# One decoder block on one core: slot weights and scatter matrix from one product, four small moves around it

## Chip, cores and metric

The kernel runs on one core of a Trainium2 chip. The metric is the device time of one launch in microseconds (us), the median over runs; lower is better.

## What is computed

One decoder layer on 256 tokens of width 1024, in float32: attention with two kinds of heads, then a mixture of 16 experts (top group of four, top two experts in it), then a final RMSNorm. The change touches the second half only:

```python
h2 = rmsnorm(x, norm2_g[l]) * (1.0 + scale2) + shift2
y = hierarchical_moe(h2, ...)          # top-1 group, top-2 experts in it
x = x + gate2 * y
return rmsnorm(x, final_g)

for e in range(N_EXPERTS):
    act = jax.nn.silu(hf @ w_gate[e]) * (hf @ w_up[e])
    out = out + combine[:, e:e + 1] * (act @ w_down[e])
```

`gate2` is one row of 1024 numbers from the conditioning vector, `combine` is zero but for a token's two experts, and `w_gate`, `w_up` and `w_down` are 96 MB together.

## The kernel before

Tokens stand in two tiles of 128 (t = 0, 1). After the router (lines 1059 to 1111) every expert has 64 slots, and the experts are worked through in eight pairs (p = 0 to 7, the loop at line 1359), a pair filling 128 slot rows. What a token's slot is stands in `onehot` (tokens x slots, zeros and ones, line 1190).

For each pair TensorE runs, in an order written by hand: the gate products (`in_half(p, "g", ...)`, line 1245) with the scatters of the pair before last between them, the up products, `slot_weights` (line 1256), the first half of the previous pair's down products (`down_rows`, line 1302), the transposes of the activations (`act_transpose`, line 1283), and the second half of the down products. After every odd pair `gather` (line 1200) fetches the tokens of the next four experts. Weights come by loads of 1 MB, all on the SP queue, into a ring of tiles (`st.tile`), many loads ahead of TensorE.

`slot_weights` makes two things for a pair. `sT` (slots x tokens) is the transpose of `onehot`, which later scatters the results back to the tokens; it is made by two TensorE transposes and copied out of PSUM by ScalarE. `ws` is one routing weight for each slot; it comes from two small float32 products of `onehot` with the routing weights `combv`, and two ScalarE copies. `weigh` (line 1320) multiplies a down product by `ws` and by the row `adaacc[5, n]` on VectorE and splits the result into a high part (`yh`) and a low part (`yl`); `scatter` (line 1338) multiplies them back into the accumulators `oacc`.

Three more places matter. `mod_rows(5)` (line 472) spreads the row `gate2` over all partitions, two float32 products and two ScalarE copies; it stands in pair 0, between `slot_weights` and `act_transpose`. `keep_clock` (line 167) issues bf16 products whose result nobody reads, three and four of them, while the router's small VectorE steps run. `final_row` (line 1132) spreads `final_g` over the partitions with eight small products and two ScalarE copies; it stands behind the last down products of pair 6. The end of the kernel is `norm_part` (line 1145, sums of squares on ScalarE and the product with `fg` on VectorE, by three column parts) and `norm_end` (line 1166): sum, power on GpSimd, scaling on ScalarE and VectorE, and four stores.

In the expert loop only TensorE's order is written by hand; in the router all of TensorE's, VectorE's and ScalarE's is. Elsewhere a scheduler sets it.

Of the kernel before, what the change touches and what calls it, by code (L numbers as in the profile page):

```python
# [61 lines left out]
def hybrid_block_kernel(  # L62
# [408 lines left out]

    def mod_rows(which):

        for j in range(2):
# [581 lines left out]
    weigh_logits(1)  # L1056
    keep_clock(3)

    larger = moe.tile([P, SETS, 16], F32, name="larger", bufs=1)
    G.memset(larger, 0.0)  # L1060
# [27 lines left out]
    h2_lo(0, 1)  # L1088
    keep_clock(4)

# [36 lines left out]
    PARTS = [slice(0, 512), slice(512, 768), slice(768, 1024)]  # L1127
    fgrow = small.tile([P, P], F32, name="fgrow", tag="lgs")[0:KD, :]
    nc.scalar.dma_start(fgrow, final_g.rearrange("(k p) -> k p", p=P))
    fg = []  # L1130
# [12 lines left out]
    norm = {}  # L1143

    def norm_part(i):
# [7 lines left out]
        for t in range(NT):  # L1153
            junk = act[:, 0:c.stop - c.start]
            S.activation(junk, oacc[t][n][:, cs], AF.Square, scale=D ** -0.5,
                         accum_out=ss[:, i, t:t + 1])
            if c is not PARTS[-1]:
                V.tensor_tensor(o[:, t, c], oacc[t][n][:, cs], fg[0][:, c], op=ALU.mult)
        if c is not PARTS[-1]:
# [6 lines left out]
    def norm_end():  # L1166
        o, ss = norm["o"], norm["ss"]
        c, cs = PARTS[-1], slice(PARTS[-1].start - FW, FW)
        r = small.tile([P, NT], F32, name="rstdf", tag="rstd")
        V.tensor_tensor(r, ss[:, len(PARTS) - 1, :], ss[:, len(PARTS) - 2, :], op=ALU.add)  # L1170
        G.tensor_tensor(r, r, mhalf, op=ALU.pow)
        for t in range(NT):
            rt_ = r[:, t:t + 1]
            S.mul(o[:, t, 0:512], o[:, t, 0:512], rt_)
            V.scalar_tensor_tensor(o[:, t, c], oacc[t][1][:, cs], rt_, fg[0][:, c], op0=ALU.mult,  # L1175
                                   op1=ALU.mult)
            V.tensor_scalar(o[:, t, 512:c.start], o[:, t, 512:c.start], rt_, None, op0=ALU.mult)  # L1177
            nc.scalar.dma_start(out[t * P:(t + 1) * P, 0:512], o[:, t, 0:512])
            nc.sync.dma_start(out[t * P:(t + 1) * P, 512:], o[:, t, 512:])
# [76 lines left out]
    def slot_weights(p):  # L1256

        lo = (2 * p) % 4
        oh = [onehot[p // 2 % 2][:, t, lo:lo + 2, :].rearrange("p e s -> p (e s)") for t in range(NT)]
        sp = psa(f"st{p}")  # L1260
        for t in range(NT):
            PE.transpose(sp[:, t * P:(t + 1) * P], oh[t].bitcast(F32), ident)
        for t in range(NT):
            PE.matmul(sp[:, T:T + NE], oh[t].bitcast(F32), combv[:, t, :], start=(t == 0),  # L1264
                      stop=(t == 1))
        sT = moe.tile([P, T], F32R, name="sT", tag="sT")
        S.copy(sT, sp[:, 0:T])  # L1267
# [69 lines left out]

    def scatter(yy, sT, n, cs):

        for y in yy:  # L1340
            for t in range(NT):
                m = sT[:, t * P:(t + 1) * P]
                PE.matmul(oacc[t][n][:, cs], m.bitcast(F32) if len(yy) == 1 else m, y, start=False,  # L1343
                          stop=True, skip_group_check=True)

    def scatter_pair(p, n, c):
        scatter(ys.pop((p, c.start)), sw[p][1], n, slice(c.start - FW * n, c.stop - FW * n))

    one_hot(0)
    for n in range(2):  # L1350
        h2_lo(1, n)
    combv = route_weights()
    by_hand.__exit__(None, None, None)
    NP = NE // 2
    whole_cols = [slice(0, FW), slice(FW, D)]
    with tc.manual_schedule(engines={PE.engine}):
        gather(0, 0)
        gather(0, 1)
        for p in range(NP):
# [17 lines left out]
            if p == 0:  # L1377
                mod_rows(5)
                nmaxi = most_tokens()
# [9 lines left out]
        load_down(p)  # L1389
        final_row()  # L1390
        scatter_pair(p - 1, 0, whole_cols[0])
# [14 lines left out]

    norm_end()

# [98 lines left out]
```

## Time and profile before

| | |
|---|---|
| median of three runs | 470.38 us (468.78 to 470.97) |
| the profiled execution, its own time | 470.29 us |
| its span, first to last instruction | 468.6 us |
| TensorE busy | 448.2 us, 96% |
| VectorE, ScalarE, GpSimd busy | 220.6, 160.6, 14.7 us |
| mean DMA rate | 338 GB/s |
| mean granted TensorE clock | 0.989 of 2.4 GHz |

The profile gives each instruction's start and length, what it waited for, and, by stretches, each engine's busy time, the granted clock (1.00 is 2.4 GHz, 0.50 is 1.2 GHz) and the DMA rate. A float32 product shows as two MATMUL rows. Since the ends of matmuls are modelled, the distance from one group's start to the next group's start tells more than their lengths.

### The profile page before, as it was taken

The numbers are of one execution on the slowest core, as the hardware profiler recorded it, in microseconds if no ns is written. First come the engines' busy times: TensorE is split into PE (matmuls) and PEld (weight loads), VectorE is DVE, ScalarE is ACT, GpSimd is POOL, SyncE is SP. The second block draws the span as 40 slices with busy tenths as digits, with TensorE's granted clock in tenths as the row PEclk, the third lists the DMA queues.
The fourth block names the chain that finished last, engine by engine and source line by source line (L and its number), as shares of the span: only waits on it lengthen the run. The fifth ranks groups of instructions, "written<-read, shape, count | busy, mean of one in ns | idle before, by whom it ended". The sixth has DMA issues, their size and how long they took to land. (4 is left out here: it accounts for less than half of the span.)

```text
span 468.6 us, 6867 instructions
## 1 busy us (share of the span) xinstructions
PE 448.2 (96%) x2724; PEld 281.2 (60%) x2724; DVE 220.6 (47%) x378; ACT 160.6 (34%) x292; POOL 14.7 (3%) x51
## 2 busy tenths in 40 slices
PE   5999999999999999999899999999999999999991
PEld 1769988976889999978453345333533335333440
DVE  5558878956999964787640030031202111020332
ACT  3543686465663444363641012011201102110222
POOL 5210000000000000000100000000000000000000
PEclk9999999999999999999999999999999999999986
DMA  8999978789797979976779999999999999999502
GB/s 290 368 324 354 295 267 287 247 287 382 254 374 255 385 263 407 422 308 219 294 258 408 424 420 418 422 419 421 420 421 419 422 419 421 420 420 404 196 0 94
DMA packets 51971, 158.46 MB, mean 338 GB/s; under 512 B 6448, under 2 KB 16728, under 8 KB 40160
## 3 DMA queue, kind: packets, MB, share of 16 engines
q1 hardware_dynamic: 51568, 157.44, 87.6%
q8 instruction: 23, 0.38, 0.3%
q10 hardware_dynamic: 368, 0.55, 0.3%
q14 instruction: 12, 0.10, 0.1%
HBM read 156.93 MB, written 1.05 MB: 337 GB/s over the span
## 5 line engine op out<-in xcount | busy, mean ns | idle before, releaser
L1252 PE MATMUL gps<-g,hg 128*64 128x512 f32 x256 | 57.9, 596 | 0.0
L1252 PE MATMUL ups<-u,hg 128*64 128x512 f32 x256 | 56.6, 595 | 0.0
L1309 PE MATMUL dps<-d,aT 128*64 128x512 f32 x224 | 51.2, 598 | 0.0
L1281 DVE TENSOR_TENSOR act<-act,ups 128x512 f32<-128x512 f32 x8 | 5.5, 687 | 93.6 <-PE ups L1252 93.6
L409 PE MATMUL g_acc<-hT,wsp 128*128 128x256 f32 x384 | 48.4, 285 | 0.3 <-DVE wsp L363 0.3
L409 PEld LDWEIGHTS g_acc<-hT,wsp 128*128 128x128 f32 x384 | 46.7, 191 | 1.6 <-issue 1.0
L1252 PEld LDWEIGHTS ups<-u,hg 128*64 128x64 f32 x256 | 17.9, 137 | 35.3 <-issue 35.3
L1252 PEld LDWEIGHTS gps<-g,hg 128*64 128x64 f32 x256 | 17.4, 137 | 33.2 <-issue 32.6
L1309 PEld LDWEIGHTS dps<-d,aT 128*64 128x64 f32 x224 | 14.8, 136 | 25.4 <-issue 25.2
L446 DVE SCALAR_TENSOR_TENSOR adarow<-adaw,cact,adarow 128x512 f32<-128x512 f32 x40 | 29.6, 743 | 0.4
L1327 ACT CAST yh<-yt 128x512 fp32r<-128x512 f32 x15 | 9.3, 618 | 56.7 <-DVE yt L1323 56.7
L1267 ACT CAST sT<-st 128x256 fp32r<-128x256 f32 x8 | 3.0, 372 | 63.4 <-PE st L1264 63.4
L940 PE MATMUL wo<-wsp,mT 128*128 128x512 f32 x96 | 23.7, 400 | 0.7 <-DVE wsp L363 0.7
L878 PE MATMUL br<-oT,wsp 128*128 128x256 f32 x192 | 23.2, 282 | 0.0
L1280 ACT ACTIVATE act<-gps 128x512 f32<-128x512 f32 x8 | 4.8, 598 | 53.7 <-PE gps L1252 53.7
L878 PEld LDWEIGHTS br<-oT,wsp 128*128 128x128 f32 x192 | 23.0, 188 | 0.2 <-DVE wsp L363 0.2
L1335 DVE TENSOR_TENSOR yl<-yt,yh 128x512 fp32r<-128x512 f32 x7 | 4.8, 692 | 34.3 <-PE oacc L1343 32.4
L940 PEld LDWEIGHTS wo<-wsp,mT 128*128 128x128 f32 x96 | 17.6, 188 | 5.2 <-DVE wsp L363 1.1
L1323 DVE SCALAR_TENSOR_TENSOR yt<-dps,ws,adarow 128x512 f32<-128x512 f32 (+1 forms) x17 | 12.2, 719 | 14.3 <-PE dps L1309 8.3
L1288 DVE COPY aT<-actT 128x512 f32<-128x512 f32 x8 | 5.5, 691 | 27.0 <-PE actT L1286 27.0
L1212 PEld LDWEIGHTS hg<-onehot,h2s 128*128 128x128 f32 x128 | 15.7, 191 | 4.2 <-ACT yh L1327 2.4
L1212 PE MATMUL hg<-onehot,h2s 128*128 128x256 f32 x128 | 16.8, 287 | 1.0 <-DVE h2s L1012 0.5
(295 smaller groups left out, 679.4 us busy)
## 6 DMA issues: line engine op xcount, KB each, us to landing
g<-in_expert_w_gate SPq DMA_DIRECT2D x32, 1024.0 KB, 14.6
u<-in_expert_w_up SPq DMA_DIRECT2D x32, 1024.0 KB, 16.3
d<-in_expert_w_down SPq DMA_DIRECT2D x30, 1024.0 KB, 17.2
adaw<-in_ada_w SPq DMA_DIRECT2D x16, 1024.0 KB, 6.4
ada<-in_ada_w SPq DMA_DIRECT2D x8, 512.0 KB, 8.9
ada<-in_ada_w SPq DMA_DIRECT2D x16, 256.0 KB, 8.5
wo<-in_w_out SPq DMA_DIRECT2D x4, 1024.0 KB, 12.9
kaw<-in_w_in SPq DMA_DIRECT2D x4, 512.0 KB, 6.6
```

Of the source, the lines that this page charges most:

```text
L409: PE.matmul(self.acc[m // 2][:, (m % 2) * T:(m % 2 + 1) * T], w[a][:, kk, m * P:(m + 1) * P], hT[b][:, k, :], start=(k == 0 and i == 0 and ...
L446: V.scalar_tensor_tensor(acc, adaw[which, j, k // 4][:, k % 4, :], cact[:, k:k + 1], acc, op0=ALU.mult, op1=ALU.add)
L878: PE.matmul(bacc[br][m // 2][:, (m % 2) * T:(m % 2 + 1) * T], wk[a][:, 0, m * P:(m + 1) * P], oT[br][b][:, k, :], start=(k == 0 and i == 0 ...
L940: PE.matmul(acc[t][n], mT[b][:, k, t * P:(t + 1) * P], ws[k // 2][a][:, k % 2, :], start=(k == 0 and i == 0), stop=(k == KD - 1 and i == 2))
L1212: PE.matmul(ps[:, kk * T:(kk + 1) * T], h2s[t][i][:, k * P:(k + 1) * P], oh[:, t].rearrange("p e s -> p (e s)"), start=(n == 0 and kk == 0 ...
L1252: PE.matmul(ps[64 * i:64 * i + 64, :], hg[:, k, (lo + i) * CAP:(lo + i + 1) * CAP], wt[nm, p][half][i][:, k % 4, :], start=(k == 0), stop= ...
L1280: S.activation(av, in_place(gu["g", p]), AF.Silu)
L1281: V.tensor_tensor(av, av, in_place(gu["u", p]), op=ALU.mult)
L1288: V.tensor_copy(aT, ap.rearrange("p (f s) -> p f s", f=KF))
L1309: PE.matmul(ys[p, FW * n][64 * i:64 * i + 64, :], aTs[p][:, 2 * h + k, 64 * i:64 * i + 64], dt_[p, h][i][:, k, FW * n:FW * n + FW], start= ...
L1323: V.scalar_tensor_tensor(y, ps, ws, adaacc[5, n][:, cs], op0=ALU.mult, op1=ALU.mult)
L1327: S.copy(hi, y)
```

## The change

A tile `wmove` is built once after the router: for each token tile 32 columns of routing weights, split in high and low parts, and one identity of 128 columns between them. `slot_weights` then needs one float32r product for each token tile, `onehot` times 160 columns of `wmove`, which gives the transpose and the weights together; two VectorE sums pick the weights of a pair out of them. Token tile 1 comes first in `sT`, so `scatter_pair` reads it in the order (1, 0). The two rows of `gate2` move to the places of `keep_clock(3)` and `keep_clock(4)`. `final_g` is spread over the partitions by one load on the SP queue behind the last weights. `norm_end` works by token tile, in an order written by hand, and the first half of tile 0's output is stored by the SP queue.

```diff
-    keep_clock(3)
+    mod_rows(5, (0,))
...
-    keep_clock(4)
+    mod_rows(5, (1,))
...
-    def final_row():
-        fg.append(st.tile("fg")[:, 0:D])
-        for n in range(2):
-            ps = psa(f"fg{n}")
-            for k in range(4):
-                PE.matmul(ps[:, k * P:(k + 1) * P],
-                          ident[0:KD, 4 * n + k:4 * n + k + 1].broadcast_to([KD, P]), fgrow,
-                          start=(k == 0), stop=True, skip_group_check=True)
-            S.copy(fg[0][:, 512 * n:512 * n + 512], ps)
...
-        V.tensor_tensor(r, ss[:, len(PARTS) - 1, :], ss[:, len(PARTS) - 2, :], op=ALU.add)
-        G.tensor_tensor(r, r, mhalf, op=ALU.pow)
         for t in range(NT):
+            V.tensor_tensor(rs[:, t:t + 1], ss[:, last, t:t + 1], ss[:, last - 1, t:t + 1],
+                            op=ALU.add)
+        for t in range(NT):
+            G.tensor_tensor(rs[:, t:t + 1], rs[:, t:t + 1], mhalf[:, 0:1], op=ALU.pow)
...
-            nc.scalar.dma_start(out[t * P:(t + 1) * P, 0:512], o[:, t, 0:512])
+            (nc.sync, nc.scalar)[t].dma_start(out[t * P:(t + 1) * P, 0:512], o[:, t, 0:512])
...
-        for t in range(NT):
-            PE.transpose(sp[:, t * P:(t + 1) * P], oh[t].bitcast(F32), ident)
-        for t in range(NT):
-            PE.matmul(sp[:, T:T + NE], oh[t].bitcast(F32), combv[:, t, :], start=(t == 0),
-                      stop=(t == 1))
+        PE.matmul(sp[:, 0:SW], oh[1], wmove[:, 2 * NE:2 * NE + SW], start=True, stop=True)
+        PE.matmul(sp[:, SW:2 * SW], oh[0], wmove[:, 0:SW], start=True, stop=True)
...
-            S.copy(ws[64 * i:64 * i + 64, :],
-                   sp[64 * i:64 * i + 64, T + 2 * p + i:T + 2 * p + i + 1])
+            V.tensor_reduce(ws[64 * i:64 * i + 64, :],
+                            sp[64 * i:64 * i + 64, P + 2 * p + i:P + 4 * NE:NE], axis=AX, op=ALU.add)
...
+    SW = P + 2 * NE
+    wmove = moe.tile([P, 2 * NE + SW], F32R, name="wmove", tag="wmove", bufs=1)
+    S.copy(wmove[:, 2 * NE:SW], ident)
...
-                mod_rows(5)
                 nmaxi = most_tokens()
                 act_transpose(p)
...
-        final_row()
+        fg = st.tile("fg")[:, 0:D]
+        nc.sync.dma_start(fg, final_g.unsqueeze(0).broadcast_to([P, D]))
```

The first place is TensorE in pair 0, from `slot_weights` to the first gate product of pair 1 (`st` holds the scatter matrix and the weights, `bc` the spread rows of `gate2`, `pmT` a transposed count, `actT` the transposed activations). Before:

```order
L1262 MATMUL st_2741<-ident,onehot_2618 128x128 x2
L1264 MATMUL st_2741<-rt_comb,onehot_2618 128x16 x2
L477 MATMUL bc_2751<-adarow_1597,onesr 128x512
L477 MATMUL bc_2754<-adarow_1608,onesr 128x512
L1119 MATMUL pmT<-ident,rt_pmax 1x128
L1286 MATMUL actT_2765<-ident,act 128x128 x4
L1252 MATMUL gps_2796<-g_0_2772,hg 64x512
```

With the change:

```order
L1253 MATMUL st_2742<-wmove,onehot_2613 128x160
L1254 MATMUL st_2742<-wmove,onehot_2613 128x160
L1120 MATMUL pmT<-ident,rt_pmax 1x128
L1276 MATMUL actT_2758<-ident,act 128x128 x4
L1242 MATMUL gps_2789<-g_0_2765,hg 64x512
```

Four instructions of `slot_weights` became two, and the two products of `mod_rows` are gone from here.

The second place is TensorE behind the last down product of pair 6 (`dps_1`); `oacc` are the scatters of pair 6 and `dps_3681` the first down product of pair 7. Before:

```order
L1309 MATMUL dps_1_3628<-d_1_3566,aT 64x512
L1138 MATMUL fg_3664<-fgrow,ident 128x128 x4
L1138 MATMUL fg_3670<-fgrow,ident 128x128 x4
L1343 MATMUL oacc_2533<-yh_2623,sT 128x512
L1343 MATMUL oacc_2567<-yh_2623,sT 128x512
L1343 MATMUL oacc_2533<-yl,sT 128x512
L1343 MATMUL oacc_2567<-yl,sT 128x512
L1297 MATMUL dps_3681<-d_0_3653,aT 64x512
```

With the change:

```order
L1299 MATMUL dps_1_3607<-d_1_3547,aT 64x512
L1333 MATMUL oacc_2533<-yh_2618,sT 128x512
L1333 MATMUL oacc_2567<-yh_2618,sT 128x512
L1333 MATMUL oacc_2533<-yl,sT 128x512
L1333 MATMUL oacc_2567<-yl,sT 128x512
L1287 MATMUL dps_3649<-d_0_3632,aT 64x512
```

The eight products of `final_row` no longer stand between the down products and the scatters.

The third place is VectorE from the weighing of pair 7's second part to the sums of the final norm (`ssf` are sums of squares, `o` the output before scaling). Before:

```order
L1323 SCALAR_TENSOR_TENSOR yt<-dps_3697,ws,adarow_1608 128x256
L1158 TENSOR_TENSOR o<-oacc_2533,fg 128x512
L1158 TENSOR_TENSOR o<-oacc_2567,fg 128x512
L1162 TENSOR_SCALAR ssf<-ssf 128x2
L1323 SCALAR_TENSOR_TENSOR yt<-dps_3718,ws,adarow_1608 128x256
L1158 TENSOR_TENSOR o<-oacc_2551,fg 128x256
L1158 TENSOR_TENSOR o<-oacc_2583,fg 128x256
L1164 TENSOR_TENSOR ssf<-ssf 128x2
L1170 TENSOR_TENSOR rstdf<-ssf 128x2
```

With the change:

```order
L1313 SCALAR_TENSOR_TENSOR yt<-dps_3665,ws,adarow_1608 128x256
L1148 TENSOR_SCALAR ssf<-ssf 128x2
L1144 TENSOR_TENSOR o<-oacc_2533,fg 128x512
L1144 TENSOR_TENSOR o<-oacc_2567,fg 128x512
L1313 SCALAR_TENSOR_TENSOR yt<-dps_3686,ws,adarow_1608 128x256
L1144 TENSOR_TENSOR o<-oacc_2551,fg 128x256
L1144 TENSOR_TENSOR o<-oacc_2583,fg 128x256
L1150 TENSOR_TENSOR ssf<-ssf 128x2
L1158 TENSOR_TENSOR rstdf<-ssf 128x1 x2
```

The small sum over `ssf` went ahead of the two products with `fg`, and the last sum is done once for each token tile.

## Rows read from the trace of the kernel before

**Rows 1.** Busy time by stretch: PE, PEld, DVE, ACT, POOL, clock, DMA, GB/s.

```profile
260.00:280.00 20.00, 20.00 (x98) 6.87 (x94) 2.90 (x6) 1.79 (x5) 0.00 (x0) 1.00 1.01 421
...
420.00:440.00 20.00, 20.00 (x94) 7.61 (x96) 2.43 (x4) 1.17 (x4) 0.00 (x0) 1.00 1.02 382
```

**Rows 2.** Timeline of PE, pairs 0 and 1: start, length, line, operation, shape, count.

```profile
254.63 0.44 PE L1262 MATMUL st<-ident,onehot 128*128 128x128 f32 x2
...
255.27 1.96 PE L477 MATMUL bc<-adarow,onesr 128*128 128x512 f32 x4
...
257.18 0.60 PE L1286 MATMUL actT<-ident,act 128*128 128x128 f32 x4
257.71 7.09 PE L1252 MATMUL gps<-g,hg 128*64 128x512 f32 x32
...
271.59 0.44 PE L1262 MATMUL st<-ident,onehot 128*128 128x128 f32 x2
...
272.31 3.65 PE L1309 MATMUL dps<-d,aT 128*64 128x512 f32 x16
...
280.07 4.09 PE L1212 MATMUL hg<-onehot,h2s 128*128 128x256 f32 x32
```

**Rows 3.** Issue of the second of the last weight loads, timeline of the SP queue.

```profile
415.19 1.13 SPq L1242 DMA_DIRECT2D d<-in_expert_w_down  x1
```

**Rows 4.** DMA issues from 414 to 417 us: count, size, us to landing.

```profile
d<-in_expert_w_down SPq DMA_DIRECT2D x1, 1024.0 KB, 20.4
```

**Rows 5.** Timeline of all engines behind the last down products of pair 6.

```profile
437.66 3.65 PE L1309 MATMUL dps<-d,aT 128*64 128x512 f32 x16
...
441.14 0.69 DVE L1330 TENSOR_TENSOR yl<-yt,yh 128x512 fp32r<-128x512 f32 x1 [0.74 <-ACT yh L1327]
...
441.25 2.05 PE L1138 MATMUL fg<-fgrow,ident 8*128 8x128 f32 x16
...
443.22 0.73 PE L1343 MATMUL oacc<-yh,sT 128*128 128x512 f32 x2
...
444.38 5.26 PE L1297 MATMUL dps<-d,aT 128*64 128x512 f32 x16
```

**Rows 6.** Timeline of all engines at the end.

```profile
454.33 1.41 DVE L1158 TENSOR_TENSOR o<-oacc,fg 128x512 f32<-128x512 f32 x2 [1.13 <-ACT act L1155]
...
454.82 0.19 ACT L1155 ACTIVATION_READ_ACCUMULATOR act<-oacc 128x1 f32 x1
...
455.76 0.48 DVE L1323 SCALAR_TENSOR_TENSOR yt<-dps,ws,adarow 128x256 f32<-128x256 f32 x1
...
457.39 1.21 PE L1343 MATMUL oacc<-yt,sT 128*128 128x256 f32 x4 [0.65 <-DVE o L1158]
...
459.44 0.70 POOL L1171 TENSOR_TENSOR rstdf<-rstdf,mhalf 128x2 f32<-128x2 f32 x1 [230.29 <-DVE rstdf L1170]
460.18 1.33 ACT L1174 ACTIVATE o<-o,rstdf 128x512 f32<-128x512 f32 x2 [1.00 <-POOLq L1411]
```

**Rows 7.** Timeline of all engines in pair 0, VectorE.

```profile
254.84 0.69 DVE L1281 TENSOR_TENSOR act<-act,ups 128x512 f32<-128x512 f32 x1 [13.53 <-PE ups L1252]
```

**Rows 8.** Timeline of all engines in the router, PE.

```profile
233.21 0.81 PE L171 MATMUL warm<-identb 128*128 128x512 bf16 x3
...
234.32 1.02 PE L171 MATMUL warm<-identb 128*128 128x512 bf16 x4
...
235.77 0.78 PE L1212 MATMUL hg<-onehot,h2s 128*128 128x256 f32 x3 [0.43 <-DVE onehot L1194]
```

**Rows 9.** Busy time, clock and DMA rate in two single microseconds, columns as in group 1.

```profile
443.00:444.00 1.00, 1.00 (x6) 0.77 (x5) 0.00 (x0) 0.97 (x3) 0.00 (x0) 1.00 0.00 0
...
445.00:446.00 1.00, 1.00 (x4) 0.24 (x2) 0.25 (x1) 0.00 (x0) 0.00 (x0) 0.50 0.00 0
```

**Rows 10.** Timeline of all engines in the router, GpSimd.

```profile
223.03 0.56 POOL L250 TENSOR_TENSOR rstd<-rstd,mhalf 128x1 f32<-128x1 f32 x1
```

**Rows 11.** All six last weight issues, timeline of the SP queue.

```profile
412.69 20.72 SPq L1242 DMA_DIRECT2D d<-in_expert_w_down  x6
```

More of the change, by code (lines that the diff above doesn't have):

```diff
@@ L470, in mod_split, with mod_rows @@
             msplit[which].append((hi, lo))
-    def mod_rows(which):
-        for j in range(2):
+    def mod_rows(which, js=(0, 1)):
+        for j in js:
             ps = psa(f"bc{which}{j}")
@@ L1056, in hybrid_block_kernel @@
     weigh_logits(1)
-    keep_clock(3)
-    larger = moe.tile([P, SETS, 16], F32, name="larger", bufs=1)
+    mod_rows(5, (0,))
+    larger = moe.tile([P, 192], F32, name="larger", tag="wmove", bufs=1)
+    larger = larger[:, 0:SETS * 16].rearrange("p (s c) -> p s c", s=SETS)
     G.memset(larger, 0.0)
@@ L1127, in hybrid_block_kernel @@
     PARTS = [slice(0, 512), slice(512, 768), slice(768, 1024)]
-    fgrow = small.tile([P, P], F32, name="fgrow", tag="lgs")[0:KD, :]
-    nc.scalar.dma_start(fgrow, final_g.rearrange("(k p) -> k p", p=P))
-    fg = []
-    def final_row():
-        fg.append(st.tile("fg")[:, 0:D])
-        for n in range(2):
-            ps = psa(f"fg{n}")
-            for k in range(4):
-                PE.matmul(ps[:, k * P:(k + 1) * P],
-                          ident[0:KD, 4 * n + k:4 * n + k + 1].broadcast_to([KD, P]), fgrow,
-                          start=(k == 0), stop=True, skip_group_check=True)
-            S.copy(fg[0][:, 512 * n:512 * n + 512], ps)
     norm = {}
@@ L1157, in norm_part @@
             if c is not PARTS[-1]:
-                V.tensor_tensor(o[:, t, c], oacc[t][n][:, cs], fg[0][:, c], op=ALU.mult)
+                V.tensor_tensor(o[:, t, c], oacc[t][n][:, cs], fg[:, c], op=ALU.mult)
         if c is not PARTS[-1]:
@@ L1168, in norm_end @@
         c, cs = PARTS[-1], slice(PARTS[-1].start - FW, FW)
-        r = small.tile([P, NT], F32, name="rstdf", tag="rstd")
-        V.tensor_tensor(r, ss[:, len(PARTS) - 1, :], ss[:, len(PARTS) - 2, :], op=ALU.add)
-        G.tensor_tensor(r, r, mhalf, op=ALU.pow)
+        rs = small.tile([P, NT], F32, name="rstdf", tag="rstd")
+        last = len(PARTS) - 1
         for t in range(NT):
-            rt_ = r[:, t:t + 1]
-            S.mul(o[:, t, 0:512], o[:, t, 0:512], rt_)
-            V.scalar_tensor_tensor(o[:, t, c], oacc[t][1][:, cs], rt_, fg[0][:, c], op0=ALU.mult,
+            V.tensor_tensor(rs[:, t:t + 1], ss[:, last, t:t + 1], ss[:, last - 1, t:t + 1],
+                            op=ALU.add)
+        for t in range(NT):
+            G.tensor_tensor(rs[:, t:t + 1], rs[:, t:t + 1], mhalf[:, 0:1], op=ALU.pow)
+        for t in range(NT):
+            r = rs[:, t:t + 1]
+            S.mul(o[:, t, 0:512], o[:, t, 0:512], r)
+            V.scalar_tensor_tensor(o[:, t, c], oacc[t][1][:, cs], r, fg[:, c], op0=ALU.mult,
                                    op1=ALU.mult)
-            V.tensor_scalar(o[:, t, 512:c.start], o[:, t, 512:c.start], rt_, None, op0=ALU.mult)
-            nc.scalar.dma_start(out[t * P:(t + 1) * P, 0:512], o[:, t, 0:512])
+            V.tensor_scalar(o[:, t, 512:c.start], o[:, t, 512:c.start], r, None, op0=ALU.mult)
+            (nc.sync, nc.scalar)[t].dma_start(out[t * P:(t + 1) * P, 0:512], o[:, t, 0:512])
             nc.sync.dma_start(out[t * P:(t + 1) * P, 512:], o[:, t, 512:])
@@ L1260, in slot_weights @@
         sp = psa(f"st{p}")
[L1261 to L1265 removed]
+        PE.matmul(sp[:, 0:SW], oh[1], wmove[:, 2 * NE:2 * NE + SW], start=True, stop=True)
+        PE.matmul(sp[:, SW:2 * SW], oh[0], wmove[:, 0:SW], start=True, stop=True)
         sT = moe.tile([P, T], F32R, name="sT", tag="sT")
[L1267 removed]
+        S.copy(sT.rearrange("p (t s) -> p t s", t=NT),
+               sp[:, 0:384].rearrange("p (t c) -> p t c", t=NT)[:, :, 0:P])
         ws = moe.tile([P, 1], F32, name="ws", tag="ws")
         for i in range(2):
[L1270 to L1271 removed]
+            V.tensor_reduce(ws[64 * i:64 * i + 64, :],
+                            sp[64 * i:64 * i + 64, P + 2 * p + i:P + 4 * NE:NE], axis=AX, op=ALU.add)
         sw[p] = ws, sT
@@ L1336, in weigh_low, with scatter @@
         ys[p, FW * n] = hi, yl
-    def scatter(yy, sT, n, cs):
+    def scatter(yy, sT, n, cs, order=(0, 1)):
         for y in yy:
             for t in range(NT):
-                m = sT[:, t * P:(t + 1) * P]
+                m = sT[:, order[t] * P:(order[t] + 1) * P]
                 PE.matmul(oacc[t][n][:, cs], m.bitcast(F32) if len(yy) == 1 else m, y, start=False,
@@ L1346, in scatter_pair @@
     def scatter_pair(p, n, c):
-        scatter(ys.pop((p, c.start)), sw[p][1], n, slice(c.start - FW * n, c.stop - FW * n))
+        scatter(ys.pop((p, c.start)), sw[p][1], n, slice(c.start - FW * n, c.stop - FW * n),
+                (1, 0))
     one_hot(0)
@@ L1352, in hybrid_block_kernel @@
     combv = route_weights()
+    SW = P + 2 * NE
+    wmove = moe.tile([P, 2 * NE + SW], F32R, name="wmove", tag="wmove", bufs=1)
+    S.copy(wmove[:, 2 * NE:SW], ident)
+    for t in range(NT):
+        hi, lo = (wmove[:, SW * t + NE * i:SW * t + NE * i + NE] for i in range(2))
+        S.copy(hi, combv[:, t, :])
+        V.tensor_tensor(lo, combv[:, t, :], hi.bitcast(F32), op=ALU.subtract)
     by_hand.__exit__(None, None, None)
@@ L1405, in hybrid_block_kernel @@
         norm_part(2)
-    norm_end()
+    with tc.manual_schedule(engines={V.engine, S.engine, G.engine}):
+        norm_end()
     nmaxv = nc.values_load(nmaxi[0:1, 0:1], min_val=0, max_val=T)
```

## Prediction

> **What bounds the kernel now.** I first read the busy time by stretch. From 260 to 440 us, the expert loop, TensorE is busy for the whole of every stretch, at a granted clock of 1.00, and the DMA queues move about 420 GB/s at a full busy share [rows 1]. Both look full, so the second view is the order in time: is TensorE waiting for weights? In the timeline of TensorE each group starts where the one before it ends: the up products of pair 1 give way to `slot_weights` at 271.59, that to the down products at 272.31, and so on [rows 2]. There is no gap that a load could explain. The third view is the loads: the second-last 1 MB load of the down weights is issued at 415.19 and lands 20.4 us later, at 435.6 [rows 3, 4]; TensorE first reads it at 444.4 [rows 5]. So weights lie ready 8.8 us ahead even at the end of the stream, and TensorE alone sets the pace from pair 0 to the last scatter. A microsecond taken off TensorE in that loop is a microsecond off the time, as long as the weights stay ahead. After it comes a chain of VectorE, TensorE, ScalarE, GpSimd and stores [rows 6], in which every link counts.
>
> **The rows of gate2 leave pair 0.** Before, the two products of `mod_rows` start at 255.27, the transposes of the activations at 257.18 and the next gate products at 257.71 [rows 2]. Without them the transposes would wait for their input, which VectorE ends at 254.84 + 0.69 = 255.53 [rows 7]. They take 257.71 - 257.18 = 0.53, so the gate products start at about 256.1: **1.6 us** earlier. The cheaper `slot_weights` of pair 0 is hidden in this wait. The rows go to the router in place of seven bf16 products that take 0.81 + 1.02 us [rows 8]; they cost 1.96 us for both [rows 2]. The second one has from 234.32 to the first gather at 235.77, which waits for VectorE's `onehot` [rows 8], and needs about 1.0: nothing. The first needs 1.0 where three products took 0.8, ahead of products that wait for the router's VectorE steps; at worst 0.2. I take 0 and keep 0.2 for the range. The ScalarE copies behind them fall into time in which it is idle, and so do the copies and subtractions that build `wmove`: nothing reads it before 254.6.
>
> **One product for each token tile.** `slot_weights` takes 272.31 - 271.59 = 0.72 us of TensorE before [rows 2]. What two float32r products of 160 columns take, no row shows. The nearest is the gather: float32r with 128 x 128 weights and 256 columns, 32 of them in 4.09 us, 0.13 each [rows 2]. Two such cost 0.26, and that saves 0.46 a pair. The other end is the rate of plain float32: each of the two products of `mod_rows` streams 512 columns in 1.96 / 2 = 0.98 us, so 160 columns cost 0.31 and two 0.61, saving 0.11 a pair. I take the gather's price, as type, weights and instruction are the same and only the columns differ. Seven pairs count (1 to 7): **3.2 us**, with 0.8 and 3.3 as ends. The Trainium skill, TensorE: Matmul & The Clock Gate, section The mechanism, speaks against so much: a weight load overlaps with a running matmul only where their row groups differ, which here they don't. By it and the skill's 128 / 1.2 ns for a load, an estimate, a gather product would need 0.21 and 32 of them 6.8 us; the trace has 4.09, so the row decides. By the rule the two products would cost 0.35, this term would be 2.6 and the time 462.3.
>
> The two weight copies move from ScalarE to VectorE sums; VectorE is busy 2.4 to 2.9 us in 20 [rows 1], and the weights are needed only by the weighing, several microseconds later: nothing.
>
> **final_row leaves TensorE.** Its products start at 441.25 and the scatters behind them at 443.22 [rows 5]: 1.97 us. In the new order the scatters follow the down products at once. Their first half has its input; the second needs `yl`, ready at 441.14 + 0.69 = 441.83, 0.58 behind 441.25, about as long as the first half takes. So the whole **1.97 us** goes, and all that came before shifts alike. The load that replaces it is 512 KB behind the last weights. At 382 GB/s [rows 1] that is 1.4 us; the old stream is at zero by 443 [rows 9], so it would land by 444.4, and VectorE's first product with `fg`, at 454.33 before [rows 6], comes at about 446.8 in the new time.
>
> **The clock.** Right behind `final_row` the granted clock falls from 1.00 to 0.50, that is from 2.4 to 1.2 GHz [rows 9], and the first down product of pair 7 takes 5.26 us for 16 rows, where the last of pair 6 took 3.65 for as many [rows 5]. What TensorE did before the fall is those small products, on 8 of its 128 rows, and scatters. Take the small ones away and only products of the kind that run all through the loop at full clock are left. I expect no fall: **1.6 us**. The other end is 0.
>
> **The end.** VectorE's two products with `fg` start at 454.33 today; in the new order a small sum stands ahead of them that waits for ScalarE's second sum, at 455.01 [rows 6]. They start some 0.85 later, and so does the weighing behind them (455.76), which then ends about 0.25 later than the products of the next part may start; the last scatters waited for those products at 457.39 [rows 6]. I charge 0.3. Against that the power: 0.70 for both tiles [rows 6], 0.56 for one [rows 10], and tile 0 no longer waits for tile 1's sum of squares, about 0.5. Scaling and stores then start 0.6 earlier. Net **0.3 us**, with -0.3 and 0.7 as ends.
>
> **Sum.** 1.6 + 3.2 + 1.97 + 1.6 + 0.3 = 8.7 us. The profiled execution took 470.29, so 461.6; it lies 0.1 below the median of the three runs, which makes 461.7.
>
> **Do the weights stay ahead?** By pair 7 TensorE is 1.6 + 3.2 = 4.8 us early, and the first down product there comes another 2.0 earlier: 444.4 - 6.8 = 437.6. The load it reads lands at 435.6. It holds by 2 us. The stream itself was at its full rate and does not move.
>
> **Rivals.**
> - *The new products are dear.* At the plain float32 rate the second term is 0.8: 461.7 + 2.4 = 464.1. For it: fewer columns than any float32r product of the trace. Against: the gather.
> - *Their weight loads are not hidden.* The old `slot_weights` was six short instructions, two transposes and two float32 products of two rows each, in 0.72 us, 0.12 each, whatever their columns. If each new product pays that and then streams 160 columns at the gather's rate, 0.08, two cost 0.40, a pair saves 0.32, and the term is 2.2: 462.7. For: the new products alternate with short work, as the old did. Against: in the gather 256 columns and a load fit into 0.13. It is the skill's rule above as a mechanism of this kernel.
> - *The clock still falls*, there or in the router, where seven bf16 products give way to two: 461.7 + 1.6 = 463.3. For: the fall came after little work, and scatters remain. Against: the same scatters stand in every pair, at a clock of 1.00.
> - *Weights become the bound.* If TensorE in truth follows the loads, the first two terms are hidden and only the last part is won: 461.7 + 4.8 = 466.5. For: 420 GB/s throughout. Against: 8.8 us of lead.
> - *Slower: `fg` arrives late.* The load is last in the SP queue; VectorE's product waits for it, the weighing stands behind that, TensorE behind the weighing. Every microsecond past 446.8 counts. The last weight issue ends at 412.69 + 20.72 = 433.4 [rows 11]; with the 20.4 us of a full queue it would land at 453.8, and the time would be 468.7. Only past 455.5 is it slower than before, by over 0.5% past 457.9. For: that queue is the slowest path here. Against: the old stream has run dry by 443, and 1.4 us of transfer follow.
>
> **Chances and range.** 0.5% (2.4 us) is about what can be told from no change. My forecast has 0.49; dear products 0.18; loads not hidden 0.08; the clock 0.12; weights 0.08; late `fg` 0.05, of which 0.03 ends within what can't be told and 0.02 past it. So faster 0.95, the same 0.03, slower 0.02. The range runs from 460.2 (the second term and the last at their ends, 0.5 together, and 1 us for the runs themselves, of which the lowest lay 1.6 under the median) to 464.6, which takes in the first three rivals and leaves out 0.13.
>
> **What would show it.** The next gate products about 1.6 us earlier behind pair 0; `slot_weights` at 0.25 to 0.3 us; no rows of `final_row`; clock 1.00 through the last down products; `fg` landing before VectorE asks for it; store issues about 8.7 us earlier. The prediction is wrong if TensorE shows waits for loads in pairs 1 to 7, if a product of 160 columns takes over 0.2 us, or if the clock falls anywhere between 230 us and the last scatter.

## The result, and the profile after

| | before | after | ratio, 95% interval |
|---|---|---|---|
| first timing, median | 470.41 us (468.78 to 470.97, 4 runs) | 463.54 us (461.32 to 464.56, 4 runs) | 0.9853 (0.9806 to 0.9900) |
| repeated, median | 468.90 us (22 runs) | 462.39 us (461.41 to 464.25, 6 runs) | 0.9858 (0.9835 to 0.9882) |
| profiled execution, its own time | 470.29 us | 461.32 us | |
| span | 468.6 us | 459.6 us | |
| mean granted clock of the span | 0.989 | 0.994 | |

The change is faster by some 1.4%, with the time inside the range that was given. In some executions of nearly every kernel here the mean granted clock of TensorE is lower than in the others (0.990 or less, not 0.991 to 0.995), and these take about 2 us longer; below, such an execution is said to have an extra fall of the clock. Of 49 executions of the kernel before, 19 were such by their times (470.3 to 471.0 us, against 468.5 to 469.1), and the one profiled ahead of the prediction was of this kind; of 10 of the changed kernel, 3 were (464.25 to 464.56). Like with like, by the medians of the executions without an extra fall, it is **468.8 against 462.3, so 6.5 us**. The forecast was 8.7 against 470.29.

The timeline of TensorE in pairs 0 and 1 after the change (start, length, line, operation, shape, count; L1253 and L1254 are the new products, L1299 the first half of pair 0's down products):

```profile
254.68 0.34 PE L1253 MATMUL st<-wmove,onehot 128*128 128x160 f32 x1
...
255.64 0.66 PE L1276 MATMUL actT<-ident,act 128*128 128x128 f32 x4 [0.40 <-DVE act L1271]
256.22 6.23 PE L1242 MATMUL gps<-g,hg 128*64 128x512 f32 x28
...
263.14 7.04 PE L1242 MATMUL ups<-u,hg 128*64 128x512 f32 x32
270.11 0.34 PE L1253 MATMUL st<-wmove,onehot 128*128 128x160 f32 x1
270.28 0.28 PE L1254 MATMUL st<-wmove,onehot 128*128 128x160 f32 x1
270.49 3.65 PE L1299 MATMUL dps<-d,aT 128*64 128x512 f32 x16
```

The gate products behind pair 0 start at 256.22 where they started at 257.71 [rows 2]: 1.49 earlier, with TensorE now waiting 0.40 for VectorE's `act`; the router gave up 0.05 of it, as `slot_weights` starts at 254.68 where it started at 254.63 [rows 2]. `slot_weights` takes 270.49 - 270.11 = 0.38, where it took 0.72 [rows 2].

The same view from the last down products of pair 6 on, and at the last scatters:

```profile
433.73 3.65 PE L1299 MATMUL dps<-d,aT 128*64 128x512 f32 x16
437.31 0.73 PE L1333 MATMUL oacc<-yh,sT 128*128 128x512 f32 x2
437.95 0.73 PE L1333 MATMUL oacc<-yl,sT 128*128 128x512 f32 x2
438.61 3.65 PE L1287 MATMUL dps<-d,aT 128*64 128x512 f32 x16
442.20 0.72 PE L1333 MATMUL oacc<-yh,sT 128*128 128x512 f32 x2
...
449.98 1.21 PE L1333 MATMUL oacc<-yt,sT 128*128 128x256 f32 x4 [0.65 <-DVE o L1144]
```

And its busy time by stretch there (PE, PEld, DVE, ACT, POOL, granted clock, DMA share, GB/s):

```profile
440.00:445.00 5.00, 5.00 (x32) 2.26 (x28) 1.63 (x3) 0.62 (x1) 0.00 (x0) 1.00 0.25 93
445.00:450.00 5.00, 4.35 (x29) 2.43 (x25) 2.66 (x6) 2.33 (x8) 0.00 (x0) 1.00 0.00 0
```

The down products of pair 6 start 437.66 - 433.73 = 3.93 earlier [rows 5]. No `final_row`; the first down product of pair 7 takes 3.65 and not 5.26 [rows 5], at a clock of 1.00. The scatters start 443.22 - 437.31 = 5.91 earlier, the last ones 457.39 - 449.98 = 7.41 [rows 5, 6]. The timelines of SP, VectorE, GpSimd and ScalarE at the end:

```profile
433.38 2.13 SPq L1390 DMA_DIRECT2D fg<-in_final_g  x1
...
437.21 0.69 DVE L1320 TENSOR_TENSOR yl<-yt,yh 128x512 fp32r<-128x512 f32 x1 [0.74 <-ACT yh L1317]
...
447.63 0.17 DVE L1148 TENSOR_SCALAR ssf<-ssf 128x2 f32<-128x2 f32 x1 [1.84 <-ACT act L1141]
447.70 1.28 DVE L1144 TENSOR_TENSOR o<-oacc,fg 128x512 f32<-128x512 f32 x2
448.90 0.48 DVE L1313 SCALAR_TENSOR_TENSOR yt<-dps,ws,adarow 128x256 f32<-128x256 f32 x1
449.50 0.93 DVE L1144 TENSOR_TENSOR o<-oacc,fg 128x256 f32<-128x256 f32 x2
...
451.52 1.06 POOL L1161 TENSOR_TENSOR rstdf<-rstdf,mhalf 128x1 f32<-128x1 f32 x2 [222.29 <-DVE rstdf L1158]
...
452.10 1.33 ACT L1164 ACTIVATE o<-o,rstdf 128x512 f32<-128x512 f32 x2 [0.35 <-POOL rstdf L1161]
```

VectorE's product with `fg` waits for ScalarE's sums (the small sum ahead of it, 447.63), not for the load of `fg`. Scaling starts at 452.10, where it was 460.18 [rows 6]: 8.08 earlier. From there to the end of the span it is 7.5 us, before 8.4; that last 0.9 was in no term of the forecast and is taken up below.

### The profile page after: what moved, and what is told of

It reads as the page before. It is cut to its first block, busy times and chain, and to the rows that moved or that the text cites. A ratio compares the mean times of both kernels' runs of the same rounds, so it can differ in the third digit from the quotient of the medians.

```text
span 459.6 us, 6762 instructions
## 1 busy us (share of the span) xinstructions
PE 440.5 (96%) x2669; PEld 275.1 (60%) x2669; DVE 223.5 (49%) x397; ACT 158.4 (34%) x277; POOL 15.1 (3%) x52
## 4 chain that ended last, share of the span: by engine, by line
PE 82%; DVE 8%; DMA 4%; ACT 2%; SPq 2%; issue 1%; POOL 0%; DVEq 0%; ACTq 0%
PE gps L1242 12%; PE ups L1242 12%; PE dps L1299 11%; PE g_acc L409 7%; PE wo L940 5%; PE br L878 4%; PE oacc L1333 4%; PE hg L1202 3%; PE vb_acc L401 3%; PE qb_acc L409 2%; PE kb_acc L409 2%; DMA ada<-in_ada_w 2%; DVE adarow L446 2%; PE ka_acc L409 2%; PE va_acc L401 2%; DMA qaw<-in_w_in 2%
## 5 line engine op out<-in xcount | busy, mean ns | idle before, releaser
L1299 PE MATMUL dps<-d,aT 128*64 128x512 f32 x224 | 51.1, 598 | 0.0
L1299 PEld LDWEIGHTS dps<-d,aT 128*64 128x64 f32 x224 | 14.8, 136 | 25.8 <-issue 24.8
```

The source lines that it names most:

```text
L1299: PE.matmul(ys[p, FW * n][64 * i:64 * i + 64, :], aTs[p][:, 2 * h + k, 64 * i:64 * i + 64], dt_[p, h][i][:, k, FW * n:FW * n + FW], start= ...
```

## The experiments

**The change once more, and each of three parts alone.** These four ran beside one set of runs of the kernel before. The first is the change unaltered.

> The changed kernel once more, unaltered, for its spread. In the profiled execution (461.3 us) the clock never fell before the end; two of the four timed ones had a lower mean clock (0.989, not 0.994) and took 464.4 to 464.6. Theory A, the clock still falls once in some executions at a place with little TensorE work: times in two clusters some 2 to 3 us apart, each with its own mean clock, about 461 to 463 and 464.5. Theory B, the spread is the DMA stream's or the launch's: times spread without any tie to the mean clock.

Measured: 462.39, ratio 0.9858 (0.9835 to 0.9882). Five of six executions stand at 461.41 to 462.54, one at 464.25 with a mean clock of 0.989. So theory A holds for the step of 2 us; the spread from 461.4 to 462.5 goes with no difference in the clock.

The kernel before with `final_g` by DMA alone:

```diff
-        final_row()
+        fg = st.tile("fg")[:, 0:D]
+        nc.sync.dma_start(fg, final_g.unsqueeze(0).broadcast_to([P, D]))
```

> The kernel before with one part of the change: final_g by one load, no products of final_row. Theory A, the small products cost TensorE's queue 1.97 us and their low work made the clock fall: 3.5 us less (466.9) where the clock stays up, 2.0 less (468.4) where it falls anyway. Rival, the fall has nothing to do with them: always 2.0 us less with the clock at 0.50 again in the first down product of pair 7.

Measured: 466.97, ratio 0.9958 (0.9942 to 0.9975). Against executions of before without an extra fall, 468.8, that is 1.9; two of twelve executions stand at 469.1 and 469.5 (mean clock 0.987 and 0.988), although `final_row` is gone.

The kernel before with the new `slot_weights`, `wmove` and the order (1, 0) in the scatters alone:

```diff
-        for t in range(NT):
-            PE.transpose(sp[:, t * P:(t + 1) * P], oh[t].bitcast(F32), ident)
...
+        PE.matmul(sp[:, 0:SW], oh[1], wmove[:, 2 * NE:2 * NE + SW], start=True, stop=True)
+        PE.matmul(sp[:, SW:2 * SW], oh[0], wmove[:, 0:SW], start=True, stop=True)
```

> The kernel before with one part of the change: one float32r product for each token tile. From the changed kernel's trace slot_weights takes 0.38 us where it took 0.72: theory, 7 x 0.34 = 2.4 us less (468.0), the whole of it visible since TensorE alone sets the pace. Rival, weights set the pace and it is hidden: 470.4. Pair 0 has no wait to hide it here, so up to 2.7 less.

Measured: 466.10, ratio 0.9935 (0.9912 to 0.9958), so 2.7 of 468.8. Here `final_row` remains, and yet the profiled execution has no fall behind it; nor has that of the next kernel, where it remains too. The timeline of TensorE in this one:

```profile
438.49 2.04 PE L1139 MATMUL fg<-fgrow,ident 8*128 8x128 f32 x16
...
441.59 3.65 PE L1298 MATMUL dps<-d,aT 128*64 128x512 f32 x16
```

The down product behind the eight products takes 3.65, and not the 5.26 of the kernel before [rows 5].

The kernel before with the rows of `gate2` in the router alone:

```diff
-    keep_clock(3)
+    mod_rows(5, (0,))
...
-    keep_clock(4)
+    mod_rows(5, (1,))
...
-                mod_rows(5)
```

> The kernel before with one part of the change: the rows of gate2 in the router in place of the seven bf16 products, nothing else. Theory, 1.5 us less (468.9), because pair 0 then waits 0.4 us for VectorE. Rival, the router loses what pair 0 wins (TensorE's clock falls there without the bf16 products): 470.4 or more, with the granted clock under 1.00 between 232 and 250 us.

Measured: 467.15, ratio 0.9965 (0.9947 to 0.9983), so 1.7. Three of eleven executions stand at 468.7 to 469.3 (mean clock 0.988 and 0.989).

What follows: `gate2` and `final_row` are worth what was forecast, the products less. And the clock's fall is an event of single executions, with `final_row` and without it. Two questions stayed: does `final_row` cause falls at all, and why do two products take 0.38?

**Does final_row make the clock fall?** The kernel before, with these products issued twice:

```diff
-            for k in range(4):
+            for k in list(range(4)) * 2:
```

> The kernel before with the eight small products that spread final_g issued twice, the second time with the same result. What is asked: whether these products, on 8 of TensorE's 128 rows, make the clock fall. The step of the prediction (they make it fall): the stretch of them is twice as long, so the clock falls right behind it in every execution; 468.85 + 1.97 for the products themselves + 1.6 for the fall = about 472.4, and the profile shows 0.50 from about 446 to 450 us. The rival (the fall is an event of single executions, wherever TensorE's products come from): 468.85 + 1.97 = about 470.8 for most executions, the profile mostly without a fall before the last scatter, and about one execution in four some 2 us higher, as in the kernel before.

Measured: 472.98 (472.27 to 473.80, 6 runs), ratio 1.0082 (1.0060 to 1.0103). No execution has a mean clock above 0.989; three stand at 472.3 to 472.5, where the step of the prediction put all of them, three another 1.3 higher. The stretch behind the doubled products, columns as above:

```profile
445.00:450.00 5.00, 5.00 (x19) 1.99 (x19) 0.69 (x1) 0.59 (x1) 0.00 (x0) 0.66 0.00 0
```

and TensorE's timeline there:

```profile
441.62 3.83 PE L1138 MATMUL fg<-fgrow,ident 8*128 8x128 f32 x32
...
446.51 5.35 PE L1297 MATMUL dps<-d,aT 128*64 128x512 f32 x16
```

Behind the doubled products on 8 of the 128 rows the clock is down at 1.2 GHz, 5.35 against 3.65 for the down product. By their mean clocks and times all six executions have a fall, though only one was profiled; behind the eight of the kernel before a fall stands in its one profile, and in neither profile of the two parts above that keep `final_row`. So the mechanism of the step holds; that it was there in every execution does not. What brought the second 1.3 us in three of the six no profile shows.

**Where do the longer executions of the changed kernel lose their 2 us?** The suspicion was the router. First, the change with both rows of `gate2` back in pair 0 and nothing in their place:

```diff
-    mod_rows(5, (0,))
...
-    mod_rows(5, (1,))
...
             if p == 0:
+                mod_rows(5)
```

> The changed kernel with both rows of gate2 back in pair 0 and no product in their place in the router, so that TensorE has nothing but the router's own short products for some 5 us there. What is asked: where the executions that are some 2 us longer lose that time. Theory A (the clock falls in the router, in some executions, because TensorE has little to do there): most or all executions are now in the longer group. Gate2 in pair 0 costs 1.7, the fall 2.0 to 2.5: 462.35 + 1.7 + 2.2 = about 466.3, and the profile shows a granted clock of 0.50 somewhere between 230 and 250 us. Theory B (the longer executions lose their time elsewhere): 462.35 + 1.7 = about 464.05 for most, a few 2 us above as before, and the clock is 1.00 from 230 us to the last scatter.

Measured: 465.88 (463.67 to 467.73, 7 runs), ratio 0.9932 (0.9908 to 0.9956); no execution has a mean clock above 0.989. The profile has the fall where theory A put it:

```profile
235.00:240.00 5.00, 3.65 (x17) 3.40 (x18) 3.97 (x11) 1.37 (x2) 0.00 (x0) 0.66 0.88 329
```

The gather and the products behind it in its timeline of TensorE:

```profile
237.08 4.91 PE L1200 MATMUL hg<-onehot,h2s 128*128 128x256 f32 x29 [0.49 <-DVE h2s L1012]
...
241.93 7.09 PE L1240 MATMUL gps<-g,hg 128*64 128x512 f32 x32
```

In this execution an idle router costs one fall, but only about 1.1 us (the first gate products at 241.93, in the changed kernel at 240.80); for a part of that time TensorE waits for VectorE. It is the fastest of the seven: the others stand 1.1 to 4.1 us higher, at mean clocks down to 0.981, and what more they lose no profile shows. Then, the change with eight more products that nobody reads:

```diff
     token_logits(0)
+    keep_clock(4)
...
     token_logits(1)
+    keep_clock(2)
...
     mod_rows(5, (1,))
+    keep_clock(2)
```

> The changed kernel with eight more bf16 products whose result nobody reads, in the router: four behind the first tile's logits, two behind the second's, two behind the second row of gate2. What is asked: whether filling TensorE there takes the longer executions away. If they come from a fall in the router: no execution above 463, all near 462.35 + 0 to 0.5 for what the products delay. If they come from elsewhere: about one in four stays 2 us higher, at about 464.4 or a little above.

Measured: 462.33 (461.35 to 463.24, 5 runs), ratio 0.9843 (0.9821 to 0.9865). One of the five, the profiled one, has the longer kind's clock, 0.990. Its stretches, columns as above, and its timeline of TensorE:

```profile
25.00:30.00 5.00, 3.31 (x17) 2.54 (x16) 4.10 (x9) 2.65 (x4) 0.00 (x0) 0.89 1.10 353
30.00:35.00 5.00, 5.00 (x32) 4.35 (x34) 1.94 (x3) 1.36 (x2) 1.06 (x2) 0.77 1.04 286
```

```profile
24.40 1.65 PE L401 MATMUL va_acc<-wsp,hT 128*128 128x512 f32 x6
27.74 1.05 PE L336 MATMUL adat<-fold,aacc 128*128 128x1 f32 x8 [1.69 <-DVE aacc L330]
28.65 2.67 PE L401 MATMUL va_acc<-wsp,hT 128*128 128x512 f32 x6
...
177.61 7.64 PE L878 MATMUL br<-oT,wsp 128*128 128x256 f32 x63
```

The same places in the changed kernel:

```profile
25.22 1.65 PE L401 MATMUL va_acc<-wsp,hT 128*128 128x512 f32 x6
26.71 0.95 PE L336 MATMUL adat<-fold,aacc 128*128 128x1 f32 x8
27.52 1.65 PE L401 MATMUL va_acc<-wsp,hT 128*128 128x512 f32 x6
...
175.56 9.66 PE L878 MATMUL br<-oT,wsp 128*128 128x256 f32 x80
```

In this execution TensorE came 0.8 us sooner to the `adat` products, waited 1.69 us for VectorE's `aacc`, and right behind that wait the clock was at 1.2 GHz for some 3 us: six products of 512 columns take 2.67 and not 1.65. About half of the loss is the wait itself (the `adat` products stand 1.03 later), the other half the clock (2.67 - 1.65 = 1.02). At 175 us it is 2.0 us late, and stays so. The edits of this kernel all lie behind 200 us. So here is one execution 2 us longer that owes it to a wait at 26 us and the fall behind it, a place that the change does not touch. That the clock can fall in the router, the run before shows; whether it does so in the longer executions of the changed kernel, or whether all of them are of this kind, five executions and one profile do not tell.

**Why do two products take 0.38 us?** The change with its two products issued twice:

```diff
+        for _ in range(2):
-        PE.matmul(sp[:, 0:SW], oh[1], wmove[:, 2 * NE:2 * NE + SW], start=True, stop=True)
-        PE.matmul(sp[:, SW:2 * SW], oh[0], wmove[:, 0:SW], start=True, stop=True)
+            PE.matmul(sp[:, 0:SW], oh[1], wmove[:, 2 * NE:2 * NE + SW], start=True, stop=True)
+            PE.matmul(sp[:, SW:2 * SW], oh[0], wmove[:, 0:SW], start=True, stop=True)
```

> The changed kernel with the two float32r products of slot_weights issued twice (tile 1, tile 0, tile 1, tile 0, the same results). What is asked: why the two take 0.34 to 0.38 us a pair, not the 0.26 taken from the gather. If every product of 160 columns costs what the pair's do (a weight load that is not hidden, or slow columns): two more cost 0.34 to 0.38 in each of the seven pairs that count, +2.4 to +2.7, so about 464.9. If the extra lies at the borders to the products beside them, with half the columns of the array, and inside a run of equal products the load is hidden: two more cost at most the gather's 0.26, at least 0.16 (160 columns at its rate), +1.1 to +1.8, so about 463.4 to 464.2.

Measured: 464.02 (462.92 to 466.13, 6 runs), ratio 0.9897 (0.9874 to 0.9919): 1.6 above the changed kernel, 0.23 for each of seven pairs. Its timeline of TensorE in pair 1:

```profile
270.17 0.34 PE L1254 MATMUL st<-wmove,onehot 128*128 128x160 f32 x1
270.35 0.27 PE L1255 MATMUL st<-wmove,onehot 128*128 128x160 f32 x1
270.46 0.27 PE L1254 MATMUL st<-wmove,onehot 128*128 128x160 f32 x1
270.57 0.27 PE L1255 MATMUL st<-wmove,onehot 128*128 128x160 f32 x1
270.78 3.65 PE L1300 MATMUL dps<-d,aT 128*64 128x512 f32 x16
```

Read the starts: 0.18 for the first, 0.11 and 0.11 in the middle, 0.21 for the last. Inside the run a product with its weight load costs no more than one of the gather; what seems dear is to come in from products of the form `128*64` and to go out to them. The weight loads of the two products in the changed kernel, pair 1, timeline of all engines:

```profile
270.10 0.19 PEld L1253 LDWEIGHTS st<-wmove,onehot 128*128 128x128 f32 x1 [0.81 <-issue]
...
270.21 0.19 PEld L1254 LDWEIGHTS st<-wmove,onehot 128*128 128x128 f32 x1
```

The second load starts 0.07 ahead of its product (270.28), while the first product runs; the first load starts with its product (270.11), none of it ahead. If it is the border that costs, the two products should stand where the form is already `128*128`, at the transposes:

```diff
-            slot_weights(p)
             if p == 0:
+                slot_weights(p)
                 nmaxi = most_tokens()
                 act_transpose(p)
             else:
                 down_rows(p - 1, 0)
+                slot_weights(p)
                 act_transpose(p)
```

> The changed kernel with slot_weights moved from in front of the first half of the down products to right in front of the transposes of the activations, in pairs 1 to 7. Nothing else moves on TensorE. What is asked: whether the 0.17 us a pair that the two products cost beyond what they cost inside a run lie at the borders to products on half the array. Theory A (the border costs it): the two products and the transposes now stand side by side and share one pair of borders, so seven pairs give back 7 x 0.17 = 1.2: 462.35 - 1.2 = about 461.2. Theory B (the first product of any new kind pays it, whatever stands beside it): no border goes, 462.35 as before.

Measured: 459.78 (459.03 to 462.38, 6 runs), ratio 0.9799 (0.9771 to 0.9827): 2.6 below the changed kernel by medians, of which the trace shows 2.1; within either group of executions that is told of at the end it is 2.1 too. Its timeline of TensorE, pair 1 and the first scatter behind pair 6:

```profile
263.12 7.04 PE L1242 MATMUL ups<-u,hg 128*64 128x512 f32 x32
269.98 3.60 PE L1299 MATMUL dps<-d,aT 128*64 128x512 f32 x16
273.52 0.34 PE L1253 MATMUL st<-wmove,onehot 128*128 128x160 f32 x1
...
273.81 0.61 PE L1276 MATMUL actT<-ident,act 128*128 128x128 f32 x4
274.35 3.65 PE L1299 MATMUL dps<-d,aT 128*64 128x512 f32 x16
...
435.23 0.72 PE L1333 MATMUL oacc<-yh,sT 128*128 128x512 f32 x2
```

The two products cost 0.29 and not 0.38. What follows the up products, now of their own form, starts 269.98 - 263.12 = 6.86 behind them, where it was 270.11 - 263.14 = 6.97; the transposes and the first half of the down products give back about 0.05 each. The scatter stands at 435.23 against 437.31, 2.08 in seven pairs, 0.30 a pair. Theory A holds, and the border costs more than the 0.17 read from the products alone, because the work on either side pays too. The Trainium skill, TensorEngine Tiling (Array Packing), section Key Properties, says that a change of tiling mode drains the engine; the runs agree as far as they go, with 0.30 us for a way in and out. Whether a drain costs it, or a weight load that cannot go ahead there, they do not part.

**What is the new end worth?** The change with the old end:

```diff
-        for t in range(NT):
-            G.tensor_tensor(rs[:, t:t + 1], rs[:, t:t + 1], mhalf[:, 0:1], op=ALU.pow)
+        G.tensor_tensor(r, r, mhalf, op=ALU.pow)
...
-    with tc.manual_schedule(engines={V.engine, S.engine, G.engine}):
-        norm_end()
+    norm_end()
```

> The changed kernel with the end of the kernel before: one power for both token tiles, the scheduler's own order behind it, all first halves stored by the ACT queue. What is asked: what the new end is worth by itself. The prediction's gains there (power 0.14, tile 0 not waiting for tile 1 0.5, so 0.6): 462.35 + 0.6 = about 462.95. The sum of the parts measured so far leaves it 0.15: about 462.5. If the new end costs: below 462.3.

Measured: 463.17 (462.59 to 464.96, 6 runs), ratio 0.9868 (0.9844 to 0.9892), 0.8 above the changed kernel. Its power and scaling in the timelines of GpSimd and ScalarE:

```profile
452.12 0.70 POOL L1157 TENSOR_TENSOR rstdf<-rstdf,mhalf 128x2 f32<-128x2 f32 x1 [222.82 <-DVE rstdf L1156]
...
452.85 1.33 ACT L1160 ACTIVATE o<-o,rstdf 128x512 f32<-128x512 f32 x2 [1.01 <-POOL rstdf L1157]
```

Scaling starts at 452.85 and not 452.10: 0.75, of which 0.60 is that the power for tile 0 no longer waits for tile 1 (451.52 against 452.12).

**Three things together**: `slot_weights` beside the transposes, the eight products in the router, and VectorE's small sum on GpSimd.

```diff
-                V.tensor_scalar(ss[:, 0, :], ss[:, 0, :], EPS, None, op0=ALU.add)
+                G.tensor_scalar(ss[:, 0, :], ss[:, 0, :], EPS, None, op0=ALU.add)
```

> The changed kernel with three things: slot_weights beside the transposes (as above), the eight bf16 products in the router that keep TensorE working there, and the small sum of the first part of the norm on GpSimd, so that VectorE's products with final_g need not wait behind it. If each is worth what was read: 462.35 - 1.2 - 0.2 = about 460.9, without executions some 2 us longer. If the borders cost nothing: about 462.2.

Measured: 460.41 (460.35 to 460.50, 5 runs), ratio 0.9802 (0.9779 to 0.9825). It is not better than the move beside the transposes alone: its scaling starts at 450.09, there at 450.02. The two additions bought nothing that can be seen; its higher median goes with the step behind the scaling that is told of at the end. None of its five executions has the extra fall, of the other's six one has; that is too few to tell.

## Why the prediction was right, and where it was not

The steps, in the profiled pair of executions and by the parts:

| step | forecast | in the two traces | measured alone |
|---|---|---|---|
| `gate2` rows leave pair 0 | 1.6 | 1.49 | 1.7 |
| one product for each token tile | 3.2 | 2.45 | 2.7, over eight pairs |
| `final_row` leaves TensorE | 1.97 | 1.97, less 0.14 | 1.9 |
| the clock | 1.6 | 1.6 | 0 without a fall on either side |
| the end | 0.3 | 0.7 | 0.8 |
| behind the scaling | none | 0.9 | open |
| sum | 8.7 | 9.0 | |

The second column adds up along the traces: 1.49 at the gate products; at the last down products of pair 6 3.93, so about 2.45 for seven pairs; at the first scatters 5.91, of which 1.97 is `final_row`, and 5.91 - 1.49 - 1.97 = 2.45 again; 0.14 lost as the two scatter halves now take 438.61 - 437.31 = 1.30 for 1.16, since `yl`, ready at 437.21 + 0.69 = 437.90, comes only just before the second half at 437.95; 1.6 for the down product at full clock; 8.08 - 7.41 = 0.67 from the last scatters to the scaling.

**Right: where the time is.** TensorE sets the pace and the weights stay ahead: nowhere in the rows above does it wait for a load, and what came off it came off the time. (The load that the prediction set beside pair 7 is the last of 1 MB, not the second-last; its times stand as read.) `gate2`, `final_row` and the cover for both held to within 0.1 or 0.2. In the router the rows also do the work of the products they replaced, as the run without either shows. With the products alone pair 0 counts as well (there is no wait for `act` that hides it): 2.7 / 8 = 0.34 a pair, and 7 of these are the 2.4 of the whole change. The load of `fg` did no harm: it is issued at 433.4, between 445 and 450 us no data moves, and no row waits for it.

**Wrong: the clock.** The step read one execution, saw the clock fall behind `final_row`, and put 1.6 us on its removal. The cause was right, as the doubled products show; but the fall comes only in some executions. Between executions without a fall its removal is worth nothing, and the changed kernel has extra falls left, 3 in 10, against 19 in 49 before, of which not all need lie behind `final_row`. Over all kernels here, without the idle router and the doubled products, it is 23 of 66 executions with `final_row` and 9 of 50 without: that points the way the step went, but takes different kernels together. So the saving is 6.5 to 6.9 us by medians and not 8.7. The time itself suffers less from this: 468.8 less the other four terms, 7.1, is 461.7 as well, and without an extra fall it is 462.3. That is no merit of the step: the base of the sum held a fall, and the term took it out again. That the first median, 463.54, lies near the 463.3 of the clock's rival is luck: it is the middle of four executions of two kinds, and none stands there; where the two longer ones lost their time no profile shows.

**Wrong in size: the new products.** 2 x 0.13 was taken from the gather, where 32 products of one form follow each other. The price inside a run was right, even a little high (0.11). What the step left out was that these two stand alone between products on half of the columns. Its own sign, `slot_weights` at 0.25 to 0.3, failed, at 0.38. The rival "their weight loads are not hidden" had 0.40 a pair and 2.2 for the term, close to 0.38 and 2.45. It charges every product, and the middle ones, with a load each, take 0.11 and not its 0.20; so its size came out right by way of a cause that holds at most at the border. The rule of the Trainium skill, TensorE: Matmul & The Clock Gate, section The mechanism, gives by the prediction's estimate 0.35 and 2.6, close too; inside a run the trace does not agree with it, for by the same estimate each product would take 0.17 there.

**Too careful: the end.** The charge of 0.3 for the new order on VectorE did not come: the weighing came 0.5 later against the scatters behind pair 7's first down product (448.90 - 442.20 = 6.70, before 455.76 - 449.57 = 6.19), and before, VectorE had 0.67 us without work behind it in which it waited for ScalarE. The rows of before, TensorE and VectorE:

```profile
449.57 0.74 PE L1343 MATMUL oacc<-yh,sT 128*128 128x512 f32 x2
...
456.92 0.93 DVE L1158 TENSOR_TENSOR o<-oacc,fg 128x256 f32<-128x256 f32 x2 [0.67 <-ACT act L1155]
```

From those scatters to the last ones it is 7.78, before 7.82. The 0.6 for the power was right: 0.67 in the traces.

Put together without the clock and without the part behind the scaling: 1.49 + 2.45 + 1.97 - 0.14 + 0.04 + 0.67 = 6.5, and 468.8 - 6.5 = 462.3, which is where most executions are.

## What to carry to other kernels

Before a stall seen in one profiled execution is priced, see whether the times of many executions fall into two groups, so that the kernel has it in some only; its removal is worth its price times its share, and not its price. A short product can be dear by what stands beside it: put it next to products that use the array in the same form, which here gave about a third of what the whole change gave, for a move of one line. A price read inside a long run of equal instructions holds inside such a run.

## What was not expected of the hardware

A way in and out of products of the form `128*128` among products of the form `128*64` costs 0.30 us at 2.4 GHz, spread over the products on both sides. The fall of the clock is a matter of single executions: behind the same eight products on 8 rows it stands in one profile (5.26 us for the down product) and not in another (3.65), and in one execution it stands behind a wait of 1.69 us, 400 us ahead of the place that was studied. The Trainium skill, TensorE: Matmul & The Clock Gate, Part 1, says that the gate watches TensorE in a rhythm of its own that does not begin with the kernel; the spread among executions agrees with that, though no run here shows the rhythm.

Open is a step of about 1.0 us behind the last scaling, in executions whose clock has no extra fall: the changed kernel at 461.3 to 461.4 or 462.3 to 462.7, the one with `slot_weights` beside the transposes at 459.0 to 459.3 or 460.3 to 460.5. The profiles place it in the stores. In six of the seven with the new end, the one store whose landing is known lands 4.0 to 4.2 us behind its issue and the span ends 7.3 to 7.6 behind the start of the scaling; in the seventh, the three things together, it is 5.2 and 8.6, while the engines' times behind the scaling are the same. The DMA issues of that one, then of `slot_weights` beside the transposes (count, size, us to landing):

```profile
out<-o SPq DMA_DIRECT2D x3, 256.0 KB, 5.2
...
out<-o SPq DMA_DIRECT2D x3, 256.0 KB, 4.2
```

With the old end it is 5.0 to 5.1 and 8.4 in five profiles, and 4.3 and 8.05 in that of the changed kernel with the old end. So the 0.9 of the table goes with such a step, 5.1 before and 4.1 after, and so does a good part of the distance between the medians of these two kernels. Why a store lands later in one execution than in another, and whether the new order of the stores makes the shorter landing more frequent, no experiment here asked.
